# Gate and up in passes of 4, 6 and 6 token tiles, operand sums issued after the next tile's norm, and a sum of its own for each half of the down projection

## The chip, the cores and the metric

One NeuronCore of a Trainium2 chip runs the whole program. The metric is the device time of one execution in microseconds (us), and lower is better. The engines are named as in the profile: PE is TensorE (PEld its weight loads), DVE is VectorE, ACT is ScalarE, POOL is GpSimd and SP is SyncE, which here issues all DMAs from one queue in program order.

## What is computed

The kernel is one step of a hybrid decoder layer on 2048 prompt tokens and 32 sample tokens of width 1024. The change touches only its last third: output projection, gated residual, RMSNorm with modulation, a SwiGLU feed-forward of inner width 2816, gated residual, final RMSNorm.

```python
x = x + g1 * jnp.einsum('bse,ed->bsd', mixed, w_out)
h = rms_norm(x, norm2_g) * (1.0 + sc2) + sh2
ff = jax.nn.silu(jnp.einsum('bsd,df->bsf', h, w_gate)) * jnp.einsum('bsd,df->bsf', h, w_up)
x = x + g2 * jnp.einsum('bsf,fd->bsd', ff, w_down)
y = rms_norm(x, final_g)
```

All inputs and outputs are float32. Every matrix operand is split into a high part in the TensorE's reduced float32 format and a low part (the rest), and a product is made of three matmuls: high by high, high by low, low by high.

## The kernel before

The instructions of each engine stand in the order in which the program issues them, and nothing reorders them. Three stages matter here.

**Output projection and norm** (`phase_out`). The loop over `n` goes through the 16 token tiles in the list `order`. For each tile `stage1` makes 48 matmuls of 512 columns (L1645 to L1647), `stage1e` adds the residual, squares and sums on ACT (L1660), makes the reciprocal root with three small POOL operations (L1662 to L1664) and scales the row on DVE (`oxn`, L1665). `stage2` of a tile comes one iteration later: PE transposes `oxn` (L1673) and DVE and ACT write `h` (L1680, L1678). After the second tile of a pair, `stage2` calls `blocks`: `combine` (L1698 to L1701) makes sums of the four quarters of the pair's `h` on DVE, and of the seven operands that result, each is split by an ACT cast (L1711) and a POOL subtraction (L1712). Four operands are split at once and three one iteration later (`rest`). They go to DRAM (`d_B`) by DMAs of 256 KB, except the first four of pass 0, which stay in `R["B"]`. A stage buffer in `R["ops"]` can be written again when its store has landed. In iteration `n`, `stage2(order[n - 1])`, with `blocks` in it, stands ahead of `stage1e(order[n])`.

**Gate and up** (`phase_ff`, up to `put_off(); settle()`). The pairs replace 8 products of quarter matrices by 7 (a Strassen scheme): each pass `p` treats `NCH[p]` columns, that is the tiles of one side of its pairs side by side: 384 (three pairs), 384, and 272 (two pairs and 16 columns of samples). In a pass there are 11 rounds `q`, each for 256 of the 2816 inner columns; a round has 14 products (7 for gate, 7 for up) of 12 matmuls, 168 in all. The weights are loaded anew in each pass (4 loads of 512 KB a round); their operands are made of sums on DVE (L1901 to L1906), an ACT cast (L1909) and a subtraction (L1911) that stands on POOL, and in the third pass for 4 of 14 on DVE. Operands are made five products ahead (`LEAD`). DVE also takes each product out of PSUM (L1990 to L2000) and multiplies gate by up (L2007).

**Down** (`phase_ff` after it). The tokens are treated in two halves of 8 tiles, samples (`t == 8`) with the second. Each half has 11 steps `q` of 256 inner rows. A step takes 8 or 9 tiles by two column halves, 6 matmuls of 512 columns each (4 for samples), and DVE adds each sum to `accs[t]` (L2118); both halves of the tokens use the same `accs`. The operands of step `q + 1` are made during step `q` (`build`, `d_build`: ACT cast L2050, POOL or DVE subtraction L2051). In the last but one step of a half `pre` multiplies `accs[t]` by the gate `g2` on DVE (L2146) and adds the residual on POOL (L2147); in the last step `last_sum`, `fin_rms` and `fin_out` add the remaining sum, norm and store the tile, in an order written out by hand (`LAST`).

Of the kernel before, what the change touches and what calls it, by code (L numbers as in the profile page):

```python
# [21 lines left out]
NCH = (384, 384, 272)  # L22
# [76 lines left out]
def hybrid_step(ctx: ExitStack, tc: tile.TileContext, i: dict, o: dict):  # L99
# [1462 lines left out]
    def phase_out(R, ff):  # L1562
# [15 lines left out]
        order = [0, 3, 1, 4, 2, 5, 6, 9, 7, 10, 8, 11, 12, 14, 13, 15]  # L1578
# [88 lines left out]
        def stage2(t):  # L1667
# [13 lines left out]
            p = min(t // 6, 2)  # L1681
            j, q = divmod(t - 6 * p, (3, 3, 2)[p])
            if j == 0:
                HELD["h"] = h
                return
            blocks(HELD.pop("h"), h, p, q)
# [17 lines left out]
        def blocks(h0, h1, p, q):  # L1704
# [14 lines left out]
            for x in range(4):  # L1719
                if p == 0:  # L1720
                    put(x, [a[:, :, qs] for a in R["B"][x]])
                else:
                    stage(x, R["ops"][x])

            def rest():
                for x in range(4, 7):
                    stage(x, R["late"][x - 4] if "late" in R else R["ops"][x - 4])
# [40 lines left out]
        def sample2():  # L1768
# [17 lines left out]
            for a, b in enumerate((hi, lo)):  # L1786
                OUT.append((d_B[2][a].rearrange("p x k n -> p (x k) n")[:, :, 256:272], b.rearrange("p x k n -> p (x k) n")))
# [29 lines left out]
        R["ops"] = [[pre.tile([128, 4, 128], F32R, name=f"op{x}{a}") for a in range(2)] for x in range(6)]  # L1817
        P, close_B = group("left")
        pre = P("fB", 1)
        R["B"] = [[pre.tile([128, 4, 384], F32R, name=f"B{x}{a}") for a in range(2)] for x in range(4)]  # L1820
        R["t"] = [P("fta", 3)]
# [7 lines left out]
        for n in range(1, 16):  # L1829
# [20 lines left out]
            stage1e(order[n])  # L1850
            if n + 1 < 16:
                load_x(order[n + 1])
# [8 lines left out]
        stage2(order[15])  # L1861
        rest()
# [5 lines left out]
    def phase_ff(R):  # L1868
# [3 lines left out]
        BO = R["B"]  # L1872
# [15 lines left out]
        def g_build(s):  # L1888
# [21 lines left out]
            eng = dve if q >= 2 * NP_ and x in (2, 5) else pool  # L1910
# [6 lines left out]
        def b_load(p, x):  # L1917
            if p < 3:
                for a, t in enumerate(BO[(7 * p + x) % 8]):
# [22 lines left out]
        P, close_g = group("left")  # L1942
        more = P("fmore", 1)
        BO += [[more.tile([128, 4, 384], F32R, name=f"B{x}{a}") for a in range(2)] for x in range(4, 8)]
        R["late"] = [[a[:, :, 128 * x:128 * x + 128] for a in BO[7]] for x in range(3)]
        for x in range(4, 7):
            b_load(0, x)
# [5 lines left out]
        R["t"].append(P("ftb", 3))  # L1953
        g_load(0, 3)
        for x in range(2):
            g_load(1, x)
        while built[0] < LEAD:
            build()
        up = P("fup", 2)
        sgp = P("fsg", 6)  # L1960
# [10 lines left out]
        def product(s):  # L1971
# [5 lines left out]
            xh, xl = (t[:, :, 0:n] for t in BO[(7 * p + x) % 8])  # L1977
# [317 lines left out]
```

## Time and profile before

| | us |
|---|---|
| median of 3 runs (lowest, highest) | 3149.79 (3147.58, 3157.39) |
| profiled execution, its own time | 3146.86 |
| profiled execution, span of the trace | 3145.0 |
| PE busy, share of the span | 2981.4 (95%) |
| last tile's transposes of `phase_out` begin | 1660.3 |
| first matmul of pass 2 | 2332.3 |
| first matmul of down | 2580.6 |
| last matmul of down | 3121.3 |

The last four times of the table count from the start of the span. A row of the timeline has start and length in us, engine, line, operation, output <- inputs, shapes and, in brackets, how long the engine had been idle and what ended that. A row of the lines view has a group's busy time, the mean length of one in ns, and the idle time ahead of the group with what ended it. A row of a table by stretches has the busy time of each engine (with instruction counts), the granted TensorE clock as a share of 2.4 GHz, and the load of the DMA engines.

### The profile page before, as it was taken

How to read it: one execution, taken by the hardware profiler on the slowest of the kernel's cores; microseconds unless marked ns; L12 is line 12 of the kernel's file. 1: busy time of each engine (PE TensorE's matmuls, PEld its weight loads, DVE VectorE, ACT ScalarE, POOL GpSimd, SP SyncE). 2: the span in 40 equal slices, each digit the busy share in tenths (PEclk: the TensorE clock that was granted, in tenths of full speed). 3: DMA queues.
4: the chain of work that ended last, by engine and by line, in shares of the span. 5: the costliest groups of instructions: out<-in, count | busy, mean ns of one | idle time of the engine just before them, and what ended most of it. 6: DMA issues, size and time to landing. Idle time of an engine off the chain costs nothing.

```text
span 3145.0 us, 46998 instructions
## 1 busy us (share of the span) xinstructions
PE 2981.4 (95%) x16898; PEld 2631.0 (84%) x16898; DVE 1776.3 (56%) x3271; ACT 1143.0 (36%) x2215; POOL 1618.9 (51%) x1279
## 2 busy tenths in 40 slices
PE   8999999999999997989986999999999999989995
PEld 4777888889999996767766999999999988878783
DVE  6424533024334334775665767767778975675567
ACT  5333422204444462463433333333334443214211
POOL 4546746301333332565545666666666664455337
PEclk9999999998798998999998999999999999999997
DMA  6555745626654427773678333633354443234322
GB/s 229 165 165 158 233 128 159 207 75 156 136 117 103 97 69 227 243 261 123 208 217 248 88 111 98 223 111 98 94 190 123 116 137 113 108 108 162 100 84 85
DMA packets 395811, 461.70 MB, mean 147 GB/s; under 512 B 51933, under 2 KB 306205, under 8 KB 392438
## 3 DMA queue, kind: packets, MB, share of 16 engines
q1 hardware_dynamic: 394648, 457.61, 48.4%
q8 instruction: 134, 2.20, 0.3%
q10 hardware_dynamic: 930, 1.07, 0.1%
q14 instruction: 99, 0.81, 0.1%
HBM read 335.79 MB, written 122.81 MB: 146 GB/s over the span
## 4 chain that ended last, share of the span: by engine, by line
PE 77%; POOL 6%; issue 5%; DVE 4%; DMA 4%; SPq 1%; ACT 1%; POOLq 0%; ACTq 0%; DVEq 0%
PE fg L1983 8%; PE fg L1980 8%; PE fg L1981 8%; PE z L521 5%; PE z L522 5%; PE z L526 5%; PE fd L2110 4%; PE fd L2111 4%; PE fd L2109 4%; PE aB L877 3%; PE aB L876 3%; PE aS L809 2%; PE aS L811 2%; POOL op L1911 2%; PE aB L861 1%
## 5 line engine op out<-in xcount | busy, mean ns | idle before, releaser
L1980 PE MATMUL fg<-B,op 128*128 128x384 f32 (+1 forms) x1848 | 579.0, 323 | 25.7 <-ACT op L1909 25.7
L1981 PE MATMUL fg<-B,op 128*128 128x384 f32 (+1 forms) x1848 | 576.0, 321 | 0.0
L1911 POOL TENSOR_TENSOR op<-s,op 128x512 fp32r<-128x512 f32 x242 | 336.6, 1405 | 261.7 <-ACT op L1909 219.1
L1980 PEld LDWEIGHTS fg<-B,op 128*128 128x128 f32 x1848 | 349.2, 189 | 30.1 <-ACT op L1909 29.7
L1983 PE MATMUL fg<-B,op 128*128 128x384 f32 (+1 forms) x1848 | 370.4, 322 | 1.1
L1981 PEld LDWEIGHTS fg<-B,op 128*128 128x128 f32 x1848 | 349.6, 189 | 0.0
L883 POOL TENSOR_TENSOR pl<-p,ph 128x512 fp32r<-128x512 f32 (+2 forms) x128 | 155.3, 1213 | 310.4 <-ACT ph L882 231.3
L521 PE MATMUL z<-w,hh 128*128 128x512 f32 x768 | 309.7, 403 | 2.3 <-ACT w L316 1.7
L1983 PEld LDWEIGHTS fg<-B,op 128*128 128x128 f32 x1848 | 306.1, 188 | 5.3 <-POOL op L1911 4.7
L522 PE MATMUL z<-w,hh 128*128 128x512 f32 x768 | 304.4, 396 | 0.9 <-DVE w L317 0.9
L2051 POOL TENSOR_TENSOR op<-raw,op 128x512 fp32r<-128x512 f32 x132 | 188.9, 1447 | 209.8 <-ACT op L2050 196.2
L2118 DVE TENSOR_TENSOR acc<-fd,acc 128x512 f32<-128x512 f32 x304 | 207.8, 689 | 154.8 <-PE fd L2111 154.5
L2110 PE MATMUL fd<-op,op 128*128 128x512 f32 x704 | 278.2, 395 | 16.5 <-POOL op L2051 16.5
L2109 PE MATMUL fd<-op,op 128*128 128x512 f32 x704 | 277.8, 395 | 10.8 <-DVE ft L2159 5.3
L1911 POOL TENSOR_TENSOR op<-raw,op 128x512 fp32r<-128x512 f32 x176 | 261.1, 1499 | 52.0 <-ACT op L1909 51.9
L815 DVE CUSTOM_DVE_ANT_0 junk<-aS,mask 128x256 f32<-128x256 f32 (+1 forms) x384 | 120.9, 364 | 290.4 <-PE aS L811 289.2
L2111 PE MATMUL fd<-op,op 128*128 128x512 f32 x704 | 277.4, 394 | 0.0
L1909 ACT CAST op<-s 128x512 fp32r<-128x512 f32 x264 | 160.3, 620 | 245.8 <-DVE s L1902 167.2
L2050 ACT CAST op<-raw 128x512 fp32r<-128x512 f32 x176 | 101.8, 621 | 306.1 <-issue 212.2
L526 PE MATMUL z<-w,hl 128*128 128x512 f32 x768 | 192.8, 393 | 0.0
L2002 ACT ACTIVATE sg<-sg 128x384 f32<-128x384 f32 (+1 forms) x132 | 65.4, 495 | 323.1 <-DVE sg L1997 323.0
L521 PEld LDWEIGHTS z<-w,hh 128*128 128x128 f32 x768 | 146.5, 191 | 35.0 <-ACT w L316 2.1
(364 smaller groups left out, 6985.8 us busy)
## 6 DMA issues: line engine op xcount, KB each, us to landing
raw<-in_w_gate SPq DMA_DIRECT2D x66, 512.0 KB
raw<-in_w_up SPq DMA_DIRECT2D x66, 512.0 KB
raw<-in_w_in SPq DMA_DIRECT2D x96, 256.0 KB
raw<-d_ff SPq DMA_DIRECT2D x44, 512.0 KB
raw<-in_w_down SPq DMA_DIRECT2D x44, 512.0 KB
d_B<-op SPq DMA_DIRECT2D x82, 256.0 KB
d_ff<-sg SPq DMA_DIRECT2D x88, 192.0 KB
ar<-in_w_ada SPq DMA_DIRECT2D x32, 512.0 KB
```

Source lines behind the costliest of these rows:

```text
L521: pe.matmul(ps, hh[:, k, :], hi[:, k, :], start=(k == 0), stop=False)
L522: pe.matmul(ps, hh[:, k, :], lo[:, k, :], start=False, stop=False)
L526: pe.matmul(ps, hl[:, k, :], hi[:, k, :], start=False, stop=(k == 7))
L1911: eng.tensor_tensor(lo, src, f32(hi), ALU.subtract)
L1980: pe.matmul(ps, hi[:, k], xh[:, k], start=(k == 0), stop=False)
L1981: pe.matmul(ps, hi[:, k], xl[:, k], start=False, stop=False)
L1983: pe.matmul(ps, lo[:, k], xh[:, k], start=False, stop=(k == 3))
L2051: (dve if idx in (3, 7) else pool).tensor_tensor(lo, src, f32(hi), ALU.subtract)
L2109: pe.matmul(ps, f[0][:, tt], d[0], start=(x == 0), stop=False)
L2110: pe.matmul(ps, f[0][:, tt], d[1], start=False, stop=False)
L2111: pe.matmul(ps, f[1][:, tt], d[0], start=False, stop=(x == 1))
L2118: dve.tensor_tensor(acc, ps, acc, ALU.add)
```

## The change

Three things are altered.

1. The passes of gate and up are 4, 6 and 6 tiles (256, 384 and 400 columns, the samples still in the last). `order` is changed to fit. In pass 0 six operands stay in SBUF rather than four, and only the seventh goes through DRAM. The buffers for passes 1 and 2 are 400 columns wide; three are there during pass 0, and five take the place of pass 0's operands when it ends, so that the operands 3 to 6 of pass 1 are loaded around that moment. The subtractions on DVE are now in pass 0, 3 of 14; pass 2 has all on POOL.
2. `blocks` is no longer called in `stage2` but after the `stage1e` that follows.
3. Down has two sets of sums, `acc[0]` and `acc[1]`, and the samples go with the first half. `acc[1]` is loaded with the residual and the second half is added upon it, with `g2` multiplied into the down weights. The first half is gated, added to its residual, normed and stored by `fin0`, one tile in each step of the second half, gate and residual on POOL. In the last two steps the tiles 3 to 7 take both steps in one PSUM sum.

```diff
-NCH = (384, 384, 272)
+NCH = (256, 384, 400)
+NT = (2, 3, 3)
+TP = (0, 4, 10)
...
-        order = [0, 3, 1, 4, 2, 5, 6, 9, 7, 10, 8, 11, 12, 14, 13, 15]
+        order = [0, 2, 1, 3, 4, 7, 5, 8, 6, 9, 10, 13, 11, 14, 12, 15]
...
             if j == 0:
                 HELD["h"] = h
-                return
-            blocks(HELD.pop("h"), h, p, q)
+            else:
+                HELD["b"] = HELD.pop("h"), h, p, q
...
+            def out(x, dst):
+                if p == 0 and x < 6:
                     put(x, [a[:, :, qs] for a in R["B"][x]])
                 else:
-                    stage(x, R["ops"][x])
+                    stage(x, dst)
...
             stage1e(order[n])
+            if "b" in HELD:
+                blocks(*HELD.pop("b"))
...
-            eng = dve if q >= 2 * NP_ and x in (2, 5) else pool
+            eng = dve if q < NP_ and (x == 5 or x == 2 and w == 0) else pool
...
-        for x in range(4, 7):
-            b_load(0, x)
+        BO[0, 6] = [more.tile([128, 4, 256], F32R, name=f"B6{a}") for a in range(2)]
...
         g_load(0, 3)
         for x in range(2):
             g_load(1, x)
+        b_load(0, 6)
...
-            if w == 1 and j == NP_ - 1 and x < 6:
-                b_load(p + 1, x + 1)
+            if w == 1 and j == NP_ - 1 and x < 6 and p == 1:
+                b_load(2, x + 1)
+            if w == 1 and q == 0 and 2 <= x < 5:
+                b_load(1, x - 2)
+            if s == 14 * NP_ - 1:
+                close_g0()
+                R["close_B"]()
+                lp = P("fbig", 1)
+                BIG.extend([lp.tile([128, 4, 400], F32R, name=f"B{x}{a}") for a in range(2)] for x in range(3, 8))
+                for y in range(3, 7):
+                    b_load(1, y)
...
-            if x > 1 and h == 0 and q == NP_ - 1:
+            if x > 1 and h == 0 and q >= NP_:
                 dve.tensor_tensor(DR[q, x], DR[q, x], g2, ALU.mult)
...
-            (dve if idx in (3, 7) else pool).tensor_tensor(lo, src, f32(hi), ALU.subtract)
+            (dve if q == 0 and idx in (3, 7) else pool).tensor_tensor(lo, src, f32(hi), ALU.subtract)
...
-        accs = [dw.tile([128, DM], F32, name=f"acc{t}") for t in range(8)]
+        acc = [[dw.tile([128, DM], F32, name=f"acc{hf}{t}") for t in range(8)] for hf in range(2)]
...
+        def fin_scale(t):
+            a = of(0, t)
+            if t == 8:
                 act.copy(a, acs[32:64])
                 dve.tensor_tensor(a, acs[0:32], a, ALU.add)
+            pool.tensor_tensor(a, a, g2 if t < 8 else g2s, ALU.mult)
+            pool.tensor_tensor(a, a, X[0, t] if t < 8 else X[0, t][0:NS], ALU.add)
...
+        def fin0(t, step):
+            if step == 0:
+                fin_load(t)
+            elif step == 3:
+                fin_scale(t)
+            elif step == 5:
+                fin_rms(0, t)
+            elif step == 7:
+                fin_out(0, t)
+
+        for q in range(ND - 2):
+            hf = q // NP_
+            for t in range(8 if hf else 9):
+                for c in range(2):
+                    down([q], t, c)
                 if t < 8:
                     build()
+                    if q == 8:
+                        dma(acc[1][t], d_x1[rows(1, t), :])
+                    if hf:
+                        fin0(q - NP_, t)
                 if t in (1, 3, 5, 7):
                     d_raw(q + 2, t // 2)
+        q = ND - 2
+        for t in range(3):
+            for c in range(2):
+                down([q], t, c)
+            for _ in range(3):
+                build()
+        LAST = (0, 3, 1, 4, 2, 5, 6, 7)
+        for n, t in enumerate(LAST):
+            for c in range(2):
+                down([q + 1] if t < 3 else [q, q + 1], t, c)
+            if n > 1:
+                fin_out(1, LAST[n - 2])
+            if n:
+                fin_rms(1, LAST[n - 1])
+        fin_rms(1, LAST[-1])
+        fin_out(1, LAST[-2])
+        fin_out(1, LAST[-1])
```

## Rows read from the trace of the kernel before

**Rows 1.** Table by stretches: length, PE, PEld, DVE, ACT, POOL, clock, DMA share, GB/s.

```profile
1444.40:1660.30 215.90, 188.40 (x885) 152.62 (x883) 138.63 (x210) 90.04 (x210) 108.81 (x112) 0.96 0.65 194
1660.30:1718.40 58.10, 37.47 (x177) 36.13 (x178) 26.80 (x35) 17.76 (x33) 30.70 (x22) 0.76 0.80 258
1718.40:2332.30 613.90, 613.90 (x3529) 613.90 (x3528) 427.49 (x547) 221.35 (x420) 408.49 (x295) 1.00 0.40 126
2332.30:2580.60 248.30, 242.19 (x1850) 234.82 (x1849) 220.06 (x328) 108.84 (x221) 163.36 (x110) 1.00 0.42 122
2334.00:2352.00 18.00, 18.00 (x146) 18.00 (x145) 14.80 (x25) 8.82 (x18) 11.65 (x9) 1.00 0.63 192
2403.58:2540.33 136.75, 132.68 (x1008) 128.16 (x1008) 122.40 (x181) 59.22 (x120) 90.80 (x60) 1.00 0.42 118
2580.60:3121.70 541.10, 513.81 (x2202) 411.87 (x2200) 335.52 (x411) 133.66 (x256) 265.50 (x199) 0.97 0.32 111
2600.00:2700.00 100.00, 100.00 (x438) 82.03 (x437) 55.30 (x76) 28.04 (x49) 45.16 (x33) 1.00 0.28 98
```

**Rows 2.** Timeline of PE in the output projection: transposes that waited.

```profile
1497.26 1.09 PE L1673 MATMUL oT<-ident,oxn 128*128 128x128 f32 x8 [1.64 <-DVE oxn L1665]
...
1617.57 1.97 PE L1673 MATMUL oT<-ident,oxn 128*128 128x128 f32 x8 [3.65 <-DVE oxn L1665]
...
1647.16 1.91 PE L1673 MATMUL oT<-ident,oxn 128*128 128x128 f32 x8 [4.14 <-DVE oxn L1665]
```

**Rows 3.** Timeline of DVE and POOL in the output projection.

```profile
1510.23 1.38 DVE L1680 TENSOR_SCALAR oh<-oT,modA,modB 128x128 f32<-128x128 f32 x4 [4.18 <-PE oT L1673]
...
1514.75 1.78 DVE L1701 TENSOR_TENSOR oc<-oh,oc 128x512 f32<-128x512 f32 x1
...
1521.91 1.75 DVE L1665 TENSOR_SCALAR oxn<-x,os 128x1024 f32<-128x1024 f32 x1 [1.97 <-POOL os L1664]
...
1623.72 1.28 POOL L1712 TENSOR_TENSOR op<-oh,op 128x512 fp32r<-128x512 f32 x1 [6.76 <-DMA d_B<-op]
```

**Rows 4.** Timeline of SP's DMA issues, then DVE, before the first pass.

```profile
1658.35 3.64 SPq L110 DMA_DIRECT2D B<-d_B  x6
...
1664.42 13.58 SPq L110 DMA_DIRECT2D d_B<-op  x8
...
1684.51 0.71 SPq L110 DMA_DIRECT2D raw<-in_w_up  x1
...
1690.52 0.69 DVE L1901 TENSOR_TENSOR s<-raw,raw 128x512 f32<-128x512 f32 x1 [17.94 <-DMA raw<-in_w_up]
```

**Rows 5.** Timeline of POOL in the third pass: a subtraction with DVE quiet.

```profile
2403.61 1.29 POOL L1911 TENSOR_TENSOR op<-s,op 128x512 fp32r<-128x512 f32 x1 [2.08 <-ACT op L1909]
```

**Rows 6.** Lines view of DVE over six rounds of the third pass.

```profile
L1906 DVE TENSOR_TENSOR s<-raw,s 128x512 f32<-128x512 f32 x12 | 16.9, 1408 | 0.0
...
L1911 DVE TENSOR_TENSOR op<-s,op 128x512 fp32r<-128x512 f32 x12 | 9.8, 814 | 9.1 <-ACT op L1909 9.1
L1904 DVE TENSOR_TENSOR s<-raw 128x512 f32<-128x512 f32 x13 | 8.8, 680 | 0.0
L1997 DVE TENSOR_TENSOR fc<-fg,fu 128x272 f32<-128x272 f32 x18 | 7.8, 433 | 0.0
```

**Rows 7.** Waits of PE in down: total us, times, longest us.

```profile
PE fd L2110 <- POOL op L2051: 16.5, 6, 4.1
PE fd L2109 <- DVE ft L2159: 5.3, 2, 4.7
```

**Rows 8.** Lines view of POOL and DVE in down.

```profile
L2147 POOL TENSOR_TENSOR acc<-acc,fx 128x1024 f32<-128x1024 f32 x16 | 44.0, 2754 | 49.8 <-DVE acc L2146 49.8
...
L2118 DVE TENSOR_TENSOR acc<-fd,acc 128x512 f32<-128x512 f32 x304 | 207.8, 689 | 154.8 <-PE fd L2111 154.5
```

**Rows 9.** Timeline of ACT and DVE after the last matmul.

```profile
3136.74 1.06 ACT L2179 ACTIVATE fsp<-acc 128x1024 f32<-128x1024 f32 x1 [1.39 <-POOL fs L2180]
...
3140.23 1.28 DVE L2189 SCALAR_TENSOR_TENSOR fsp<-acc,fs,fgb 128x1024 f32<-128x1024 f32 x1 [0.72 <-POOL fs L2181]
```

More of the change, by code (lines that the diff above doesn't have):

```diff
@@ L1817, in phase_out @@
         R["ops"] = [[pre.tile([128, 4, 128], F32R, name=f"op{x}{a}") for a in range(2)] for x in range(6)]
+        R["t"] = [P("fta", 3)]
+        R["fs"] = P("fs", 6)
         P, close_B = group("left")
         pre = P("fB", 1)
-        R["B"] = [[pre.tile([128, 4, 384], F32R, name=f"B{x}{a}") for a in range(2)] for x in range(4)]
-        R["t"] = [P("fta", 3)]
+        R["B"] = [[pre.tile([128, 4, 256], F32R, name=f"B{x}{a}") for a in range(2)] for x in range(6)]
         R["close"] = [close_b, close_a]
@@ L1941, in phase_ff @@
         yield
-        P, close_g = group("left")
+        P, close_g0 = group("left")
         more = P("fmore", 1)
-        BO += [[more.tile([128, 4, 384], F32R, name=f"B{x}{a}") for a in range(2)] for x in range(4, 8)]
-        R["late"] = [[a[:, :, 128 * x:128 * x + 128] for a in BO[7]] for x in range(3)]
-        for x in range(4, 7):
-            b_load(0, x)
+        BO[0, 6] = [more.tile([128, 4, 256], F32R, name=f"B6{a}") for a in range(2)]
+        R["late"] = [[more.tile([128, 4, 128], F32R, name=f"late{x}{a}") for a in range(2)] for x in range(3)]
         yield
@@ L1956, in phase_ff @@
             g_load(1, x)
+        b_load(0, 6)
         while built[0] < LEAD:
             build()
-        up = P("fup", 2)
-        sgp = P("fsg", 6)
+        up = Q("fup", 2)
+        sgp = Q("fsg", 6)
+        big = Q("fbig", 1)
+        BIG = [[big.tile([128, 4, 400], F32R, name=f"B{x}{a}") for a in range(2)] for x in range(3)]
         OFF = []
@@ L2081, in phase_ff @@
         fg = dw.tile([128, DM], F32, name="fgb")
-        spare = [dw.tile([128, DM], F32, name=f"fsp{x}") for x in range(2)]
-        fsp = P("fs", 6)
+        asm, g2s = (dw.tile([128, DM], F32, name=f"fsp{x}")[0:NS] for x in range(2))
         smf = P("fsm", 4)
         xo = P("fx", 3)
+        while built[0] < 14 * NG + 8:
+            build()
         for x in range(4):
@@ L2089, in phase_ff, with down @@
         dma(fg, i["final_g"].rearrange("(o d) -> o d", o=1).to_broadcast([128, DM]))
-        while built[0] < 14 * NG + 8:
-            build()
         bank = [0]
-        def down(q, t, c, raw=False):
+        def down(qs, t, c):
             bank[0] ^= 1
@@ L2099, in down @@
             cs = slice(c * 512, c * 512 + 512)
+            todo = [(q, x) for q in qs for x in range(2)]
             if t == 8:
-                for x in range(2):
+                for y, (q, x) in enumerate(todo):
                     for a in range(2):
-                        pe.matmul(ps[0:64], DO[q, "s", x], DO[q, 2 + x, c][a], start=(x == 0 and a == 0), stop=(x == 1 and a == 1))
-                acc, ps = acs[:, cs], ps[0:64]
+                        pe.matmul(ps[0:64], DO[q, "s", x], DO[q, 2 + x, c][a], start=(y == 0 and a == 0),
+                                  stop=(y == len(todo) - 1 and a == 1))
+                to, ps = acs[:, cs], ps[0:64]
@@ L2105, in down @@
             else:
                 tt = slice(t % 4 * 128, t % 4 * 128 + 128)
-                for x in range(2):
+                for y, (q, x) in enumerate(todo):
                     d, f = DO[q, 2 + x, c], DO[q, x, t // 4]
-                    pe.matmul(ps, f[0][:, tt], d[0], start=(x == 0), stop=False)
+                    pe.matmul(ps, f[0][:, tt], d[0], start=(y == 0), stop=False)
                     pe.matmul(ps, f[0][:, tt], d[1], start=False, stop=False)
-                    pe.matmul(ps, f[1][:, tt], d[0], start=False, stop=(x == 1))
```

154 lines of the change are left out of this document (41 added, 113 removed).

## The prediction

> **What bounds the kernel now.** I read the page first, then a table by stretches, then the waits of PE inside the stretches that are not full. The page shows PE as by far the busiest engine, so what can be won is PE's idle time and the end without matmuls. The table says where it lies [rows 1]. Passes 0 and 1 are full from 1718.4 on: 3528 matmuls of 384 columns in 613.9 us, 29.23 us a round. The third pass is not: its six middle rounds take 22.79 us each, while an undisturbed piece of it has 146 matmuls in 18.0 us, cut ones included, which is 0.125 a step or 21.0 a round. Before the first pass 58.1 us hold a single round. Down has 2200 matmuls in 541.1 us, which at its undisturbed step (438 in 100 us, 0.2283) would be 502.3, and 23.3 us of span come after it. The output projection (215.9 us) stops at the transposes of single tiles [rows 2].
>
> **Part A, sums behind the norm.** PE's transposes wait for `oxn`. Four of the waits, on the first tile of a pair, are like the one at 1497.26 (1.64 us); two later ones of that kind are 3.65 and 4.14 [rows 2]. In all these iterations the sums stand on DVE ahead of the norm, from the end of `oh` at 1511.6 to 1516.5, about 5 us [rows 3]. The change puts them behind it, so `oxn` comes about 5 us earlier, more than any of these waits. Removed: 4 x 1.64 + 3.65 + 4.14 = 14.4 us. What is late next is the second tile of the pair: the moved step has 4 DVE operations, 4 casts on ACT and 4 subtractions on POOL, and then 8 stores on SP; behind them are queued the next tile's split and `oh` on DVE, and its loads on SP. DVE had 4.18 us idle there, waiting for PE [rows 3], and the moved 5 us mostly fit. The three operands of `rest` still wait for the stores (a POOL wait of 6.76 us [rows 3]), and `h` waits for them; hence I leave the other waits as they are. Bounds: 8 us won (the early four and little else) to 18 (the clock, 0.96 over this stretch [rows 1], comes back too).
>
> **Part B, the passes.** Columns and matmuls are the same in number. The step grows by (0.2283 - 0.1740)/128 = 0.42 ns a column [rows 1], so 400 columns take 0.181 us, 30.4 a round, and 256 take about 0.118, 19.8 a round.
>
> Entry: before, six loads of 768 KB for pass 0 went out at 1658.35, ahead of the last stores, whose eight issues then took 13.58 us; the up weights were asked for only at 1684.5 and DVE got them at 1690.5, 30.2 us after the last transposes [rows 4]. Two smaller loads now stand behind the weights. The issues alone free 3.6 us, the shorter queue perhaps as much again; I take 6.2 (3.6 to 10). From 1690.5 to the end of the round passed 27.9 us; now 11 products are left of a shorter round.
>
> Pass 0 takes over the third pass's part of the short round. In that pass DVE never waited for PE: 122.40 us busy in six rounds is 20.4, and the remaining 2.4 are almost all waits for ACT's casts, 9.1 us in six rounds at the moved kind of subtraction alone [rows 1, 6]. So DVE's queue sets the 22.8. The change takes one of four subtractions off it (0.81, and 0.76 of waiting [rows 6]) and 16 columns off some 18 operations (0.3). It adds one to POOL, 1.29 us with DVE quiet [rows 5]. That is not free for DVE: the same kind of operation with two operands in SBUF takes 680 ns in one place and 1408 in another, where POOL is at work [rows 6]. I charge 0.5, between nothing and 1.29. Pass 0: 22.8 - 1.87 + 0.5 = 21.4 a round, with bounds at PE's own 19.8 and at 23.3 (rival 1). Pass 2 of 400 columns has 30.4 us for the same operations that fitted in 29.23, so no stall. At the end of pass 0 operands 3 to 6 of pass 1 (6.3 MB) are loaded; operand 3 is wanted after 6 products of 2.1 us, and at the 258 GB/s of the entry [rows 1] its 1.6 MB take 6.1 us. I cost it at nothing; without that cover up to 5 us once.
>
> Sum of B: before 27.9 + 613.9 + 248.3 = 890.1. After: 2.1 (from the weights to the product, as before) + 11 x 21.4/14 + 10 x 21.4 + 11 x 29.23 + 11 x 30.4 = 888.8. With the entry's 6.2 the gain is 7.5 us, bounds -13 and 23.
>
> A rule of the Trainium skill speaks against this part. What the rows show is the 680 against 1408 ns [rows 6]. The page "SBUF — State Buffer", section "Who interferes with whom", says that a VectorE instruction with two SBUF inputs and a GpSimd instruction that reads SBUF use one shared port, and that the later one is blocked until the first is done. By that rule, handing a subtraction from DVE (0.68) to POOL (1.29) lengthens what goes through the port; it is rival 1, worked out there from rows. That DVE and POOL both still had idle time in the round speaks against a strict form of it.
>
> **Part C, down.** Four stops go, and what takes their place is small.
> 1. Start, half boundary and last step: PE waited 16.5 us in six waits for POOL's subtractions [rows 7], two at each place. At the start POOL was behind from the third pass; a pass of 400 columns leaves it no debt, so I take 0.5 us. At the boundary and the end the cause is `pre`: a POOL addition of 2.75 us for each tile, 16 of them [rows 8], in a step of 16 x 6 x 0.2283 = 21.9 us. The first half's finishing is now two such operations in a step, for nine steps. POOL's step in the second half: 8 x 1.29 + 2 x 2.75 + 1 for the root = 17 us of 21.9 [rows 5, 8]; cover gone, it is rival 4. DVE has 16 x 0.69 [rows 8], two multiplications of the down weights (2 x 2.3, as the same shape in L2146 has) and one output row: 17 us. Both under PE. SP: the store of `fin_out` stands ahead of one weight load a step, which has the next three tiles as cover.
> 2. The last operands: eight of them are now made in three tiles of step 20, 8.2 us, and the fourth needs a load, a multiplication, a cast and a subtraction after one another. I expect PE to wait 2.7 us there, bounds 1 and 7 (the present stop).
> 3. The last step's waits for DVE, 5.3 us and more [rows 7], came from multiplying and adding each tile by `g2` and residual after the sum. Both are gone: two DVE operations of 0.69 a tile against 2.7 us of matmuls or more.
> 4. The end. 23.3 us passed after the last matmul because DVE was several tiles behind. Now one tile: 0.5 to drain, 0.69 for the sum [rows 8], 1.25 for square and reading [rows 9], 0.9 on POOL, 1.3 + 1.3 for two output rows [rows 9], 3.5 from the last of them to the end (3145.0 - 3141.5 [rows 9]), less overlap: 8.6 us. Bounds 8 and 12.
>
> After: 502.3 + 0.5 + 2.7 + 8.6 = 514.1, against 541.1 + 23.3 = 564.4. Gain 50.3, bounds 41 and 55.
>
> **Sum.** 14.4 + 7.5 + 50.3 = 72.2 us. The profiled execution had 3146.9 (span 3145.0 and 1.9 around it), so it would have 3074.7. The median of the runs is 2.9 above that execution: 3077.6, given as 3077.
>
> **The rivals.**
> 1. Pass 0 is bound by what DVE and POOL share. Through it go, at undisturbed lengths, 10 x 1.29 + 8 x 0.68 + 4 x 0.68 + 4 x 0.43 = 22.8 us a round in the third pass (ten POOL subtractions, eight DVE sums, four DVE subtractions, four gate by up), which is just the round. For: that equality. Against: POOL and DVE both wait for ACT in that round. In pass 0 it becomes 11 x 1.29 + 8 x 0.68 + 3 x 0.68 + 4 x 0.41 = 23.3 [rows 5, 6], 1.9 more than I take, over 10.8 rounds 20 us: 3098.
> 2. The waits of part A move to the pairs' second tiles, because stores and `rest` now start later and `h` hangs on them. For: the 6.76 us wait for stores [rows 3]. Against: in the early pairs DVE has room. Gain of A 0: 3092.
> 3. Slower: in pass 0 every POOL subtraction stops DVE for its whole length. DVE's quiet round there is 14 x 0.42 for products out of PSUM (433 ns with 16 columns more [rows 6]), 8 x 0.68 + 3 x 0.68 for sums and subtractions, 4 x 0.41 for gate by up, 15.0 us, and 1.6 of waits for ACT; with 11 x 1.29 on top it is 30.8, or 9.4 above what I take, 101 us over 10.8 rounds: 3178. The change ends slower once the round needs over 28.1 us (72.2/10.8 above 21.4). Against: in the third pass the same account gives 15.9 quiet and 2.4 of waits, 18.3 of 22.8, so POOL's 12.9 us cost DVE 4.5, about a third, which is also the measure of my 0.5 for 1.29.
> 4. It doesn't do what it says in down: `fin0`'s work on POOL holds up the next operands, and the stop at the boundary is spread over nine steps. If each POOL operation also waits out a DVE operation of 0.69, a step of the second half has 8 x (1.29 + 0.69) + 2 x (2.75 + 0.69) + 1 = 23.7 us of POOL [rows 5, 8], 1.8 above PE's 21.9; 16 us come back: 3093. Against: two of DVE's three kinds of work there read PSUM or run once a step.
>
> **How the numbers follow.** Chances: the forecast 0.61, rival 1 0.20, rival 2 0.09, rival 4 0.07, rival 3 0.03. The forecast's own range is 3062 to 3090. Down to 3056 if pass 0 runs at PE's pace (16 us) and the rest of A comes; up to 3104, which takes in rivals 1, 2 and 4 and leaves room for the stop at pass 1. A measurement can tell about 0.3% (9 us) from no change. Faster 0.95, same 0.02, slower 0.03.
>
> **What the profile after will show.** Right: the transposes of the pairs' first tiles no longer wait; a round of pass 0 takes 21 to 22 us and passes 1 and 2 29.2 and 30.4; no wait at the boundary of the halves; under 10 us after the last matmul. Wrong: waits of the same size at the second tiles (rival 2), DVE or POOL with no idle time in pass 0 at 23 us or more (rival 1), waits for L2051's successor in each step of the second half (rival 4), or a stop at the start of pass 1, which I cost at nothing.

## The result, and the profile after

The changed kernel takes 3110.4 us (median of 4 runs, 3104.8 to 3114.8) against 3153.6 (3147.6 to 3157.5) for the kernel before, a ratio of 0.9864 with a 95% interval of 0.9838 to 0.9890. It is faster, by 43 us or 1.4%; 72 were forecast, and 3110 lies outside the range of 3056 to 3104.

The profiled execution took 3112.3 us (span 3110.5), 34.6 less than that of before. The table by stretches of the kernel after, in the order output projection, entry and first round, rest of pass 0, five of its rounds, pass 1, pass 2, an undisturbed piece of down's second half, all of down, and the ten us of it with the last operands; the columns are those of [rows 1].

```profile
1450.70:1657.70 207.00, 184.76 (x886) 150.46 (x884) 126.29 (x210) 89.41 (x210) 98.67 (x112) 0.96 0.70 204
1657.70:1700.20 42.50, 27.76 (x177) 26.97 (x178) 26.20 (x35) 16.05 (x31) 26.14 (x18) 0.69 0.91 298
1700.20:1928.00 227.80, 218.91 (x1683) 204.63 (x1682) 201.29 (x291) 97.76 (x200) 167.03 (x111) 1.00 0.43 127
1727.76:1841.76 114.00, 109.43 (x840) 102.29 (x841) 100.74 (x146) 48.95 (x100) 83.94 (x55) 1.00 0.40 116
1928.00:2250.50 322.50, 322.50 (x1850) 322.50 (x1849) 225.93 (x290) 116.71 (x222) 216.94 (x156) 1.00 0.44 140
2250.50:2586.80 336.30, 336.30 (x1851) 336.29 (x1850) 220.58 (x285) 117.56 (x224) 215.39 (x157) 1.00 0.35 105
2930.00:3030.00 100.00, 100.00 (x438) 82.02 (x437) 68.89 (x85) 26.00 (x48) 78.39 (x57) 1.00 0.36 127
2586.80:3101.30 514.50, 508.43 (x2201) 409.72 (x2199) 296.79 (x386) 125.55 (x243) 283.90 (x241) 0.99 0.34 120
3059.00:3069.00 10.00, 7.74 (x16) 4.75 (x17) 4.93 (x7) 3.59 (x7) 7.49 (x6) 0.51 0.08 32
```

Set against the forecast, stage by stage (the last column is what the forecast lacked):

| stage, us | before | forecast | after | lacking |
|---|---|---|---|---|
| up to the first tile's transposes | 1444.4 | 1444.4 | 1450.7 | 6.3 |
| output projection | 215.9 | 201.5 | 207.0 | 5.5 |
| last transposes to the end of the first round | 58.1 | 42.9 | 42.5 | -0.4 |
| ten rounds of pass 0 | 292.3 | 214.0 | 227.8 | 13.8 |
| pass 1 | 321.6 | 321.5 | 322.5 | 1.0 |
| pass 2 | 248.3 | 334.4 | 336.3 | 1.9 |
| down, first to last matmul | 541.1 | 505.5 | 514.5 | 9.0 |
| after the last matmul | 23.3 | 8.6 | 9.2 | 0.6 |

The first row is not of the change: up to there both kernels issue the same instructions, with another tile in second place, and in the profiles of the variants below this point lies anywhere from 1438.2 to 1455.1. Without it the traces give 40.9 us of gain, which fits the 43 of the medians. So there are three gaps to explain: 13.8 us in pass 0, 9.0 in down, 5.5 in the output projection.

**Pass 0.** A round takes 22.8 us, as it did in the third pass of before. Early in every round, at about the fourth of its 14 products, PE waits for a cast of ACT, and in the next round again at the same place (1750.55, 0.54 us). The same wait stands in the third pass of before, where the waits of PE from 2325 to 2585 count nine of them, 5.1 us in all. PE's timeline of after, then of before, then that line of the waits of before (total us, times, longest us):

```profile
1727.76 0.39 PE L1993 MATMUL fg<-B,op 128*128 128x256 f32 x1 [0.55 <-ACT op L1918]
```

```profile
2403.58 0.39 PE L1980 MATMUL fg<-B,op 128*128 128x272 f32 x1 [0.51 <-ACT op L1909]
```

```profile
PE fg L1980 <- ACT op L1909: 5.1, 9, 0.6
```

**The entry.** Its 42.5 us are the forecast's 42.9, but made up otherwise. Timeline of SP and DVE of after, beside [rows 4]:

```profile
1661.77 6.76 SPq L112 DMA_DIRECT2D d_B<-op  x8
...
1674.67 0.71 SPq L112 DMA_DIRECT2D raw<-in_w_up  x1
...
1679.94 0.69 DVE L1910 TENSOR_TENSOR s<-raw,raw 128x512 f32<-128x512 f32 x1 [10.02 <-DMA raw<-in_w_up]
```

The eight stores begin 4.1 us after the last transposes in both kernels, so the 3.64 us of loads that no longer stand ahead of them gave nothing. The stores' own issues shrank from 13.58 to 6.76 us. DVE has the up weights 22.3 us after the last transposes (30.2 before, 24.0 forecast), and the rest of the round then takes 20.3 us (18.9 forecast).

**Down.** PE waits nowhere but for 0.6 us at the start (2589.95) and at the last operands. First PE's waits from 2586 to 3110 (us in total, times, longest), then the timeline of DVE, POOL, SP and PE there:

```profile
PE fd L2130 <- ACT op L2072: 4.4, 2, 3.8
PE fd L2131 <- POOL op L2073: 1.7, 3, 0.6
```

```profile
3050.40 6.06 DVE L2179 SCALAR_TENSOR_TENSOR fx<-fsp,fs,fgb 32x1024 f32<-32x1024 f32 x1 [2.26 <-POOL fs L2173]
3056.39 1.27 DVE L2137 TENSOR_TENSOR acc<-fd,acc 128x512 f32<-128x512 f32 x2
3057.59 1.20 DVE L2069 TENSOR_TENSOR raw<-raw,g2b 128x1024 f32<-128x1024 f32 x1
...
3060.58 1.35 DVE L2069 TENSOR_TENSOR raw<-raw,g2b 128x1024 f32<-128x1024 f32 x1 [0.60 <-DMA raw<-in_w_down]
...
3050.34 5.04 POOL L2073 TENSOR_TENSOR op<-raw,op 128x512 fp32r<-128x512 f32 x4
...
3056.49 0.34 SPq L112 DMA_DIRECT2D out_y_sample<-fx  x1
3056.87 0.42 SPq L112 DMA_DIRECT2D raw<-in_w_down  x1
...
3059.57 0.79 PE L2130 MATMUL fd<-op,op 128*128 128x512 f32 x1 [3.78 <-ACT op L2072]
```

DVE's output row of the sample tile, 1.28 us for the four times larger tile at the end, takes 6.06 while POOL runs four subtractions without a pause. DVE's queue stands behind it: the evictions, and then the two multiplications by `g2` from which the last operands are made. PE stops for 4.2 us from one matmul to the next at 3059.57, then three times for 1.2 to 1.4. Behind the first stop the granted clock is 0.51 (3059 to 3069 in the table), the lower of its two levels, and a matmul of 512 columns takes 0.43 us where it took 0.23. From 3055.39 to 3069.64 the 18 matmuls take 14.3 us, and at the undisturbed step 4.1.

**The end** is as forecast: one sum, a square, one row behind the last matmul. Timeline of DVE of after:

```profile
3101.69 0.69 DVE L2137 TENSOR_TENSOR acc<-fd,acc 128x512 f32<-128x512 f32 x1 [2.07 <-PE fd L2132]
...
3105.49 1.28 DVE L2179 SCALAR_TENSOR_TENSOR ft<-acc,fs,fgb 128x1024 f32<-128x1024 f32 x1 [0.72 <-POOL fs L2173]
```

**Output projection.** PE's transposes still wait six times for `oxn` (21.6 us in all, where nine waits of before had 25.2), and now all six stand at the pairs' second tiles. Before, those of the last three pairs had 2.13, 0.96 and 7.66 us. PE's timeline of after, then of before at these three tiles:

```profile
1513.52 1.09 PE L1675 MATMUL oT<-ident,oxn 128*128 128x128 f32 x8 [0.52 <-DVE oxn L1667]
...
1601.31 1.62 PE L1675 MATMUL oT<-ident,oxn 128*128 128x128 f32 x8 [4.41 <-DVE oxn L1667]
...
1633.12 1.76 PE L1675 MATMUL oT<-ident,oxn 128*128 128x128 f32 x7 [5.41 <-DVE oxn L1667]
...
1657.67 1.54 PE L1675 MATMUL oT<-ident,oxn 128*128 128x128 f32 x6 [10.28 <-DVE oxn L1667]
```

```profile
1601.41 1.09 PE L1673 MATMUL oT<-ident,oxn 128*128 128x128 f32 x8 [2.13 <-DVE oxn L1665]
...
1633.73 1.09 PE L1673 MATMUL oT<-ident,oxn 128*128 128x128 f32 x8 [0.96 <-DVE oxn L1665]
...
1660.31 1.97 PE L1673 MATMUL oT<-ident,oxn 128*128 128x128 f32 x8 [7.66 <-DVE oxn L1665]
```

### The profile page after: what moved, and what is told of

It reads as the page before. It is cut to its first block, busy times and chain, and to the rows that moved or that the text cites. A ratio compares the mean times of both kernels' runs of the same rounds, so it can differ in the third digit from the quotient of the medians.

```text
span 3110.5 us, 46990 instructions
## 1 busy us (share of the span) xinstructions
PE 2992.2 (96%) x16898; PEld 2637.4 (85%) x16898; DVE 1712.1 (55%) x3222; ACT 1128.4 (36%) x2197; POOL 1636.9 (53%) x1324
## 4 chain that ended last, share of the span: by engine, by line
PE 78%; DVE 6%; POOL 4%; issue 4%; DMA 4%; ACT 1%; SPq 0%; POOLq 0%; ACTq 0%; DVEq 0%
PE fg L1996 8%; PE fg L1994 8%; PE fg L1993 8%; PE z L523 5%; PE fd L2131 5%; PE fd L2132 5%; PE fd L2130 5%; PE z L524 5%; PE z L528 5%; PE aB L879 3%; PE aB L878 3%; PE aS L811 2%; PE aS L813 2%; PE aB L863 2%; PE acc L928 1%
## 5 line engine op out<-in xcount | busy, mean ns | idle before, releaser
L1993 PE MATMUL fg<-B,op 128*128 128x256 f32 (+2 forms) x1848 | 578.1, 323 | 19.4 <-ACT op L1918 19.1
L1994 PE MATMUL fg<-B,op 128*128 128x256 f32 (+2 forms) x1848 | 575.9, 322 | 0.0
L1920 POOL TENSOR_TENSOR op<-s,op 128x512 fp32r<-128x512 f32 x253 | 356.7, 1425 | 234.5 <-ACT op L1918 195.4
L1996 PE MATMUL fg<-B,op 128*128 128x256 f32 (+2 forms) x1848 | 375.0, 325 | 4.2 <-POOL op L1920 2.4
L2073 POOL TENSOR_TENSOR op<-raw,op 128x512 fp32r<-128x512 f32 x174 | 230.3, 1347 | 202.7 <-ACT op L2072 198.5
L2137 DVE TENSOR_TENSOR acc<-fd,acc 128x512 f32<-128x512 f32 x326 | 221.4, 689 | 200.8 <-PE fd L2132 199.8
L1920 POOL TENSOR_TENSOR op<-raw,op 128x512 fp32r<-128x512 f32 x176 | 260.9, 1498 | 67.3 <-ACT op L1918 67.2
L2015 ACT ACTIVATE sg<-sg 128x256 f32<-128x256 f32 (+2 forms) x132 | 65.2, 494 | 337.0 <-DVE sg L2010 336.9
```

The costliest lines, as they stand in the source:

```text
L1920: eng.tensor_tensor(lo, src, f32(hi), ALU.subtract)
L1993: pe.matmul(ps, hi[:, k], xh[:, k], start=(k == 0), stop=False)
L1994: pe.matmul(ps, hi[:, k], xl[:, k], start=False, stop=False)
L1996: pe.matmul(ps, lo[:, k], xh[:, k], start=False, stop=(k == 3))
L2073: (dve if q == 0 and idx in (3, 7) else pool).tensor_tensor(lo, src, f32(hi), ALU.subtract)
L2137: dve.tensor_tensor(to, ps, to, ALU.add)
```

## The experiments

Each variant is the changed kernel with one edit, unless it says otherwise. A round of pass 0 is measured from the first matmul of its second round to that of pass 1, by ten. The totals of single runs carry the early stretch's variation (17 us over the profiles), so verdicts on a stage go by the stage's own time.

### What sets pass 0's round

Three theories for 22.8 us. *DVE's queue*, as in the forecast: the round is what DVE has to do, so a subtraction more or less on DVE moves it up or down, and operands built earlier change nothing. *The shared port*, rival 1: the sum of what goes through it, so a subtraction moved from POOL (1.29) to DVE (0.68) shortens the round. *Cover*, formed after seeing the wait above: operands are built five products ahead in program order, and that is too few while DVE, ACT and POOL hand them on.

Four subtractions of 14 on DVE:

```diff
-            eng = dve if q < NP_ and (x == 5 or x == 2 and w == 0) else pool
+            eng = dve if q < NP_ and x in (2, 5) else pool
```

> In pass 0 four of 14 subtractions on DVE again (both of the third operand, both of the sixth), nothing else changed. A round of pass 0 takes 22.8 us with three. If DVE's queue sets the round (the working of the prediction): 1.4 more, 24.2. If what DVE and POOL share sets it: 1.29 - 0.68 = 0.6 less, 22.2. If it is lead lost at the turn of a round (a burst of sums on DVE, then POOL's subtractions one after another): about unchanged, 22.5 to 23.1, with the wait moved from the products fed by POOL to those fed by DVE.

Measured: 22.59 us a round, 3110.5 in total. None on DVE (`eng = pool`):

> In pass 0 all 14 subtractions on POOL. DVE's queue: three times 1.4 less, so PE's own pace, 20.0 us a round. Shared port: 3 x 0.6 more than 22.8, 24.6. Lead: POOL's train grows from five or six to eight subtractions at about 1.6 us, 23.5 to 25.

Measured: 23.48 us, 3115.6. Both edits speak against DVE's queue (24.2 and 20.0) and against the port's sum (22.2 and 24.6). The first lies in the range given for lead, the second just under it. Six products ahead instead of five:

```diff
-        LEAD = 5
+        LEAD = 6
```

> Operands made six products ahead rather than five, nothing else changed. The engines' work in a round is the same. If DVE's queue or the shared port sets the round of pass 0: unchanged at 22.8 us. If it is lead that is lost at the turn of the round: 1.4 us less or more than that, 20.0 to 21.4, some 15 to 30 us over the pass. Passes 1 and 2 unchanged at 29.3 and 30.6.

Measured: 21.63 us (1697.3 to 1913.7 for ten), 3096.8, and PE's recurring wait for ACT is gone. Lead was to bring at least 1.4 us, and it brings 1.15. Neither of the first two theories allows that: the same work on the same engines runs faster because it is handed out one product earlier. DVE's rows over five rounds, after and then with six ahead (busy us, mean ns of one, idle before):

```profile
L2020 DVE TENSOR_TENSOR sg<-fc,sg 128x256 f32<-128x256 f32 x20 | 16.0, 800 | 1.1 <-ACT sg L2015 1.1
L1920 DVE TENSOR_TENSOR op<-raw,op 128x512 fp32r<-128x512 f32 x10 | 15.4, 1535 | 3.3 <-ACT op L1918 3.3
...
L1911 DVE TENSOR_TENSOR s<-s,raw 128x512 f32<-128x512 f32 x10 | 11.8, 1181 | 0.3
```

```profile
L1911 DVE TENSOR_TENSOR s<-s,raw 128x512 f32<-128x512 f32 x10 | 16.7, 1668 | 0.3
L1920 DVE TENSOR_TENSOR op<-raw,op 128x512 fp32r<-128x512 f32 x10 | 14.4, 1442 | 0.0
...
L2020 DVE TENSOR_TENSOR sg<-fc,sg 128x256 f32<-128x256 f32 x20 | 10.2, 508 | 0.7 <-ACT sg L2015 0.2
```

With six ahead, the wait of 3.3 us in five rounds ahead of DVE's subtractions is gone, and gate by up no longer falls beside POOL's subtractions (508 against 800 ns), while one sum falls beside them more often (1668 against 1181). So the edit also changes which operations of DVE fall beside POOL's, a rival to lead as the cause. Seven ahead, the most that eight operand slots allow:

> The changed kernel with LEAD = 7 (operands of the passes built seven products ahead, the most that eight operand slots allow). If with LEAD = 6 the round of pass 0 (21.63 us) is still short of cover, it falls further, to 20.3 to 21.2 us (14 products of 12 x 0.119 give 20.0). If from LEAD = 6 on it is the work of DVE, ACT and POOL that sets the round, it stays at 21.5 to 21.7; if the slot that is now filled right behind its last matmul makes ACT wait for PE, it grows to 22 or more.

Measured: 21.63 us again, 3096.9. Gate by up falls beside POOL's subtractions again and takes longer than it did at five ahead:

```profile
L2020 DVE TENSOR_TENSOR sg<-fc,sg 128x256 f32<-128x256 f32 x21 | 18.8, 896 | 0.5
```

The round stays short all the same, so the place of this operation is not what six ahead gained. Cover is used up at six, and something else sets 21.6. To see which, the split is varied at six ahead (together with the edit of down's last operands below):

> LEAD = 6, five tiles of step 20 alone, and four of a round's 14 subtractions of pass 0 on DVE instead of three. With LEAD = 6 the round was 21.6 us with POOL waiting 5 us in it for ACT's casts and then running trains of subtractions at 1.5 to 1.7 us each, longer than a product of 1.43. If these trains set the round, one subtraction less on POOL takes it to 20.4 to 21.1 us and the total to 3083 to 3093. If DVE's own queue sets it, a subtraction more (0.68 quiet, 1.45 beside POOL) makes it 22.3 to 23.0 and the total 3098 to 3108. If PE's 20.0 plus fixed waits set it, it stays at 21.6.

Measured: 22.34 us a round, where the same kernel with three on DVE has 21.64. At six ahead a subtraction more on DVE costs 0.7 us; at five ahead it had won 0.2. The five rounds of six ahead, then of six ahead with four on DVE (columns of [rows 1]):

```profile
1718.81:1827.35 108.54, 107.48 (x843) 102.00 (x842) 98.83 (x146) 49.24 (x100) 87.67 (x56) 1.00 0.42 122
```

```profile
1710.45:1822.57 112.12, 107.42 (x843) 102.07 (x841) 103.38 (x151) 49.22 (x100) 80.32 (x51) 1.00 0.40 118
```

DVE is busy 19.77 and 20.68 us a round and idle 1.94 and 1.75. Its busy time grew by 0.91 and the round by 0.7, with POOL relieved by 1.5. That is what DVE's queue would do, and neither the port's sum nor POOL's trains would; the total, 3097.0, lies 1 us under the range given for it. It is not shown beyond that, as PE waits again in each round of this variant, 0.4 us for ACT's cast and 0.5 for POOL, where with three on DVE it waits 0.1. So cover may be short there once more, and seven ahead with four on DVE was not run.

### The last operands of down

Theories for the stop at 3059.57: DVE's late multiplications, behind the row that POOL stretched; the weight load, which stands on SP behind the store of that row; POOL's number of subtractions in step 20. First the load ahead of the finishing work in each step:

```diff
                 if t < 8:
                     build()
                     if q == 8:
                         dma(acc[1][t], d_x1[rows(1, t), :])
-                    if hf:
-                        fin0(q - NP_, t)
                 if t in (1, 3, 5, 7):
                     d_raw(q + 2, t // 2)
+                if t < 8 and hf:
+                    fin0(q - NP_, t)
```

> In each step of the second half the next weights' load is asked for ahead of the finished tile's store, nothing else changed. If PE's stop at the last operands hangs on that load (issued at 3056.9 behind the samples' store, 0.6 us of DVE's wait): the gaps of 4.2, 1.3, 1.2, 1.4 us lose 0.6 to 3 us. If it hangs on DVE, whose output row waited 6.1 us in the way of POOL's four subtractions: unchanged within 0.7 us.

Measured: the four gaps are 4.16, 1.34, 1.21 and 1.35 us, down 514.6, total 3114.1. The load is not it. Next the sample tile's row, moved behind the second tile of the last step:

```diff
-            elif step == 7:
+            elif step == 7 and t < 8:
                 fin_out(0, t)
...
+            if n == 1:
+                fin_out(0, 8)
             if n:
                 fin_rms(1, LAST[n - 1])
```

> The changed kernel, with the row operation of the sample tile (fin_out of tile 8, DVE) and its store moved from the end of step 19 to behind the second tile of the last step. If that operation, stretched to 6.06 us beside POOL's four subtractions, is what makes the last operands late, the first of the four gaps (4.17 us) shrinks to under 2 us and the half clock behind it goes; first to last matmul of down falls from 514.5 to 508 to 511 us. If the operands are late because POOL has too many subtractions in step 20, the gaps stay as they are, and down stays at 514 to 515.

Measured: the gaps are 1.85, 1.35, 1.32 and 1.36, down 511.5, total 3113.0. Three of the nine us come back, half a us fewer than the least expected, and the half clock stays (0.66 from 3060 to 3070). The trace shows why the rest does not come back: the next DVE operation in the queue now meets the same four subtractions. DVE and POOL of this variant:

```profile
3054.64 5.56 DVE L2069 TENSOR_TENSOR raw<-raw,g2b 128x1024 f32<-128x1024 f32 x1
...
3054.07 5.04 POOL L2073 TENSOR_TENSOR op<-raw,op 128x512 fp32r<-128x512 f32 x4
```

The multiplication by `g2`, 1.20 us above, takes 5.56. Last, more time for the chain, with five tiles of step 20 ahead of the last step instead of three, and the same builds behind the first three:

```diff
-        for t in range(3):
+        for t in range(5):
             for c in range(2):
                 down([q], t, c)
-            for _ in range(3):
+            for _ in range(3 if t < 3 else 0):
                 build()
-        LAST = (0, 3, 1, 4, 2, 5, 6, 7)
+        LAST = (0, 1, 5, 2, 3, 6, 4, 7)
...
-                down([q + 1] if t < 3 else [q, q + 1], t, c)
+                down([q + 1] if t < 5 else [q, q + 1], t, c)
```

> In step 20 of down five tiles alone rather than three, so that the last operands are wanted 5.4 us later; tiles 5 to 7 take both steps in one sum; the order of the last step is 0, 1, 5, 2, 3, 6, 4, 7. The changed kernel stops PE there four times (gaps of 4.2, 1.3, 1.2 and 1.4 us) and has the clock at half for some 10 us. If the stop is the lateness of the last operands: the gaps fall to 3 us or less in all, the clock stays, and down takes 505 to 507 us from first to last matmul where it took 514.5. If four more sums on DVE weigh more: the end after the last matmul grows from 9.2 us by 2 or more.

Measured: down 508.2, total 3099.7; the gap of 4.2 us is gone, two of 1.1 and 1.4 are left, and the tail stays at 9.2. The clock did not stay, as was expected: it is 0.83 from 3055 to 3065, and down is 1 us longer than the range. So 6.3 of the 9.0 us lacking were lateness of these operands. The other 2.7 were not separated.

### The output projection

The sums back ahead of the norm, alone:

```diff
-                HELD["b"] = HELD.pop("h"), h, p, q
+                blocks(HELD.pop("h"), h, p, q)
...
-            if "b" in HELD:
-                blocks(*HELD.pop("b"))
...
-        blocks(*HELD.pop("b"))
```

> The second part of the change undone alone: the operand sums stand ahead of the next tile's norm again. From the first tile's to the last tile's transposes the output projection takes 215.9 us before and 207.0 after. If moving the sums gave that: about 216 here, with waits of 2 us at the pairs' first tiles and the second tiles' (4.8 and 5.8 us after) smaller. If the other order of tiles and the fewer stores at the start gave it: about 207.

And the opposite, the kernel before with only this part of the change:

> The kernel before with the second part of the change alone: sums behind the next tile's norm. Its output projection takes 215.9 us. By the prediction's working the early four waits and two later ones go: 201.5. By what the changed kernel shows (waits moved to the second tiles): 207 to 211.

Measured, from the first tile's transposes to the last's, first the changed kernel with the sums ahead, then the kernel before with the sums behind:

```profile
1445.40:1660.30 214.90, 188.64 (x885) 152.62 (x883) 137.93 (x210) 89.79 (x210) 107.86 (x112) 0.96 0.68 195
```

```profile
1455.10:1662.90 207.80, 186.01 (x885) 151.49 (x883) 126.79 (x210) 89.25 (x210) 98.33 (x112) 0.95 0.69 203
```

214.9 against 207.0, and 207.8 against 215.9: the part is worth 8 us both ways, and does it by itself. Undoing it also takes the last three waits from 4.41, 5.41 and 10.28 us to 2.08, 1.61 and 6.84, so it is the moved sums that lengthen these. The totals, 3114.5 and 3148.5, show little of it, since single runs differ by more.

Where the other 5.5 of the expected 14.4 went: up to iteration 12 two of the three operands of `rest` get stage buffers of their own and the third another one, so that stores hold them up less:

```diff
-                    out(x, R["late"][x - 4] if "late" in R else R["ops"][x - 4])
+                    out(x, R["late"][x - 4] if "late" in R else R["ops"][x - 4 if R["n"] > 12 else (4, 5, 0)[x - 4]])
...
+            R["n"] = n
```

> The three late operands of a pair go into buffers that are not waiting for the pair's stores (two of them, up to iteration 12), nothing else changed. If the waits that are left at the pairs' second tiles (0.9 us in three early pairs, 4.8 at 1601, 5.8 at 1633) hang on those stores: the early ones and the one at 1601 go, 2 to 6 us of the 207 us; the one at 1633 (iteration 13) and the last stay. If they hang on DVE's own work (sums and the samples' small operations): unchanged within 1 us.

Measured: 206.5 us for the stage (total 3114.4). ACT's waits for stores up to 1590 fall from four, 5.3 us in all, to one of 1.0. Still the early pairs' tiles take the same times as in the changed kernel, 12.3 and 13.0 in turn, and the wait at 1601 stays at 4.4. So neither the small waits at the second tiles nor that one are for stores. At the small ones DVE's `oh` waits for a POOL subtraction of the pair before (1505.37 below), which comes later now that the sums do. At 1601 DVE has the samples' small operations ahead of `oh`, without a pause from 1584.5 to 1593.5; five of them take 1.10 to 1.12 us beside POOL's work, where the others of the same shape take 0.19. DVE of the changed kernel ahead of PE's wait at 1513.52, then ACT, POOL and DVE ahead of that at 1633.12, then POOL and DVE ahead of that at 1657.67:

```profile
1505.37 1.37 DVE L1682 TENSOR_SCALAR oh<-oT,modA,modB 128x128 f32<-128x128 f32 x4 [4.41 <-POOL B L1714]
...
1622.69 0.62 ACT L1713 CAST op<-oh 128x512 fp32r<-128x512 f32 x1 [8.46 <-DMA d_B<-op]
...
1623.65 1.30 POOL L1714 TENSOR_TENSOR op<-oh,op 128x512 fp32r<-128x512 f32 x1 [6.35 <-DMA d_B<-op]
...
1624.99 1.37 DVE L1682 TENSOR_SCALAR oh<-oT,modA,modB 128x128 f32<-128x128 f32 x4 [10.80 <-POOL op L1714]
...
1648.96 1.26 POOL L1714 TENSOR_TENSOR op<-oh,op 128x512 fp32r<-128x512 f32 x1
...
1650.25 1.37 DVE L1682 TENSOR_SCALAR oh<-oT,modA,modB 128x128 f32<-128x128 f32 x4 [4.87 <-POOL op L1714]
```

Ahead of 1633.12 a cast waits 8.46 us until a stage buffer's store has landed; a subtraction follows, then `oh`, which DVE held back 10.80 us for it, then the norm, and PE's transposes come 5.41 us late. Whether buffers of their own would free that tile, too, was not tried. Ahead of 1657.67 no store stands: ACT's casts followed DVE's moved sums at once, POOL made four subtractions without a pause from 1644.91 to 1650.22, and `oh` waited for the last of them, the first operand of `rest`. There it is the moved sums themselves that stand ahead of the tile.

### Both gains together

Six ahead and five tiles, in one kernel:

> The changed kernel with LEAD = 6 and with five tiles of step 20 alone ahead of the last step, both together. If the two gains are of different stretches they add: about 12 us in the first pass's rounds and 6 in down, 3090 to 3096 us beside 3110 for the changed kernel, 0.981 to 0.984 of the kernel before. If one of the two single runs owed its gain to the early stretch, which varies by itself, it comes out at 3097 to 3104.

Measured: 3099.7 us (median of 5, 3088.3 to 3103.2) beside 3153.2, a ratio of 0.9825 with an interval of 0.9809 to 0.9842. The profiled execution, the fastest of the five, has 21.64 us a round and down in the shorter form. Its table from the first round's end to pass 1, and for down:

```profile
1694.47:1910.89 216.42, 214.35 (x1683) 203.78 (x1682) 196.93 (x292) 99.00 (x201) 175.68 (x110) 1.00 0.45 134
2569.60:3077.30 507.70, 505.86 (x2201) 408.72 (x2200) 298.09 (x389) 125.22 (x242) 284.79 (x241) 1.00 0.34 121
```

The stages add: 11.4 us in pass 0 and 6.8 in down (507.7 first to last matmul), 18.2 together. The medians differ less, by 10.7 (beside their own runs of before by 10.3: 53.5 against 43.2 gained). So the total is in the second of the ranges expected, but not for the reason given there, as both gains are in the trace in full. The spread of the five runs, 15 us, is nearly that of the early stretch, and the medians can't settle the rest. The variant with four on DVE has 3097.0 (3089.6 to 3101.2), 0.9832 (0.9817 to 0.9848) of the kernel before, no different by that measure, though its pass 0 is 7 us longer: its first transposes came at 1438.2, against 1444.3. Both are faster than the changed kernel by the stages; by the totals their intervals overlap its own by a little.

## Why the prediction was wrong

**Part A, 8.9 us instead of 14.4.** Right: the four waits of the pairs' first tiles are gone (those tiles take 12.3 instead of 14.1 us, 7.1 in all). The step that failed is "hence I leave the other waits as they are". The early pairs' second tiles got 0.6 longer three times. The two later waits of [rows 2] were put into the sum whole (7.8), but over the last seven tiles only 3.7 came back, because the second tiles' waits there grew from 2.13, 0.96 and 7.66 us to 4.41, 5.41 and 10.28. `h` waits for a subtraction behind the moved sums, which the prediction had only for stores. Rival 2 named the place and the path, but gave it the whole gain of the part and put it down to stores as well: stores held `h` up at 1633 alone, and separate buffers changed nothing at the early pairs and at 1601.

**Part B, the entry: the number right, in part by luck.** 42.5 us against 42.9 forecast. The up weights came 1.7 us sooner than forecast, and the products behind them took 1.4 longer. The 3.6 us that the loads' issues were to free are not there; all that was won came from the shorter issues of the stores, which the forecast had at "perhaps as much again".

**Part B, pass 0: 22.8 instead of 21.4 us, 13.8 in all.** The step that failed: "So DVE's queue sets the 22.8". It was drawn from DVE's waits alone, as DVE never waited for PE. But PE waited for ACT's cast in the same rounds (2403.58 above, nine times in that pass), and the working leaves these waits out. DVE, ACT, POOL and PE form a loop there, and the loop had too little lead. Then work taken off DVE becomes waiting: forecast were 19.8 us busy and 1.6 of waits, measured 20.15 and 2.65. With six ahead it is 19.77 and 1.94 over five rounds, so both terms were about right for a kernel whose operands are early enough; 1.15 of the 1.38 us a round that were lacking are lead, and 0.2 is size. PE's own pace, a bound of the range, was worked out as 19.8; the step given, 0.42 ns a column, makes it 20.1. Rival 1 came closest with its 23.3 and 3098, but for a reason that the runs refute. That the sum of quiet lengths equals the third pass's round, 22.8, was a coincidence: in pass 0 it is 23.3, more than the round; with the split changed the round went to 22.59 and 23.48, not to the 22.2 and 24.6 that its steps give; and with six ahead the round fell to 21.63 while the sum stood still. The rule of the page "SBUF — State Buffer" (section "Who interferes with whom") in the Trainium skill was weighed with that rival. The trace agrees that such operations are stretched, 680 to some 1450 or 1670 ns; that this sets the round it does not show. In down, such an operation was held through four of POOL's and not through one (the last section). Rival 3, 30.8 us, did not happen.

**Passes 1 and 2: 322.5 and 336.3 against 321.5 and 334.4.** Full, as forecast, and no stop at the start of pass 1. A matmul of 384 columns took 29.32/168 = 0.1745 us, of 400 columns 0.182; the steps taken were 0.3 and 0.5% short.

**Part C, 40.7 us instead of 50.3.** Right: no wait at the half boundary, POOL busy 78.4% in the second half (17 of 21.9 us, 78%, forecast), rival 4 not there, the tail 9.2 against 8.6. The step that failed is "the last operands": 2.7 us with bounds 1 and 7. The 18 matmuls there took 10.2 us more than their undisturbed step gives, in four gaps of 8.1 us from matmul to matmul and at the lower clock (0.51) behind the first of them, which the forecast had at nothing. I counted the chain of load, multiplication, cast and subtraction at their undisturbed lengths, and did not see that DVE's queue ahead of it could be held for 6 us by POOL's four subtractions.

**The range.** It was bounded by mechanisms taken one at a time, with the expected value of all others. Three terms came out on the slow side together, and the early stretch, which the medians carry, was not in it: 3 us of the forecast were for the difference between the profiled execution and the median, while the spread is 17.

## What to carry to other kernels

Before calling an engine the bound of a loop from its own busy time and waits, read who waits for whom all around the loop, PE first: a wait that recurs in every round, however short, can mean that the loop lacks lead, and then work taken off an engine can turn into waiting, as it did here; varying the lead by one tests that in one run. An operation off the critical path that shares its engine with the chain of the last operands belongs in the price of that chain, at the length it has beside the other engine's work. Sum such gains from the stages, and judge a version by the stages too where a stretch that nobody touched varies by more than the gain.

## What the runs showed of the hardware

A DVE operation that reads two operands in SBUF can wait for a whole queue of POOL operations, not for one. Twice it met four subtractions of POOL that ran without a pause for 5.04 us, as different operations (a row of 32 partitions, a multiplication of 128), and both times it ended 1.08 to 1.09 us after the last of them (3056.46 after 3055.38, and 3060.20 after 3059.11): it took 6.06 and 5.56 us, where a row of 128 partitions took 1.28 at the end and a multiplication 1.20 at 3057.59. In pass 0, sums of half the multiplication's size took 1.45 to 1.67 us instead of 0.68, not much more than one POOL operation, and POOL's slowed down from 1.29 to between 1.5 and 1.74. DVE, then POOL of the changed kernel:

```profile
1744.23 1.67 DVE L1911 TENSOR_TENSOR s<-s,raw 128x512 f32<-128x512 f32 x1
...
1747.59 1.45 DVE L1910 TENSOR_TENSOR s<-raw,raw 128x512 f32<-128x512 f32 x1
...
1738.94 1.74 POOL L1920 TENSOR_TENSOR op<-s,op 128x512 fp32r<-128x512 f32 x1
...
1747.00 1.49 POOL L1920 TENSOR_TENSOR op<-s,op 128x512 fp32r<-128x512 f32 x1
```

What makes the difference between the two patterns wasn't tried.

The time to the first transposes of the output projection, 1438.2 to 1455.1 us over the profiles of kernels with the same instructions up to there, was a surprise in its size, half a per cent of the whole.
